# Two weight tiles a visit, in place of one, for the modulation's columns on TensorE

## The chip, the core and the metric

The kernel runs on one core of one Trainium2 chip. The metric is the device time of one execution in microseconds. A core has the engines TensorE (PE; its weight loads are listed apart as PEld), VectorE (DVE), ScalarE (ACT), GpSimd (POOL) and SyncE (SP), which here only issues loads and stores. Each engine works through its own instructions in the order in which they were put down at build time, and semaphores hold an instruction until what it reads is there.

## The reference

A trunk of two layers on 1024 tokens of 1024 channels. Layer 0, in which the change lies, mixes tokens by a Conformer convolution:

```python
c_act = jax.nn.silu(c)
for i in range(DEPTH):
    mod = c_act @ ada_w[i] + ada_b[i]
    sh_m, sc_m, g_m, sh_f, sc_f, g_f = jnp.split(mod, N_ADA, axis=-1)
    h = modulate(rms_norm(x, norm_mix_g[i]), sh_m, sc_m)
    # i = 0: u = a * sigmoid(g) with [a, g] = h @ w1 + b1; causal depthwise
    # convolution of width 31; LayerNorm; silu; @ w2 + b2   (i = 1: pooling)
    x = x + (1.0 + g_m)[:, None, :] * y
    h = modulate(rms_norm(x, norm_ffn_g[i]), sh_f, sc_f)
    x = x + (1.0 + g_f)[:, None, :] * swiglu_ffn(h, ...)
```

`modulate(h, shift, scale)` is h * (1 + scale) + shift. The change is about `c_act @ ada_w[0]` for the last four of the six parts of mod (g_m, sh_f, sc_f, g_f), of 1024 columns each.

## The kernel before, in words

The tokens are worked on in two chunks of 512, A and B. Every large product is made of three products of a high and a low part; a block of 24 products (8 tiles of input channels, 3 products each) makes one output tile of 128 channels by 512 tokens in a PSUM bank. In conv_in, blocks a and g come in turn: a_92 and g_93 (in PE's order by their ids a_715, g_716), then a_127 and g_128 (a_854, g_855), then a_982 with g_983, a_1105 with g_1106, and so on. ScalarE makes t, the sigmoid of a g, DVE multiplies it by a into u, and with that both banks are free again. t_124 is the sigmoid of g_93, t_141 that of g_128. Beside this DVE and GpSimd work through the 31 taps of the depthwise convolution on u: DVE adds its taps up in ca, and for GpSimd ScalarE makes the products pr, which GpSimd adds up in pa; in the end DVE adds pa to ca. There are three buffers for pr.

While chunk A is in conv_in, chunk B's norm is made. TensorE sums the squares (var), DVE takes the reciprocal root (var, col), TensorE spreads it over the partitions (rstd), and for each of eight tiles DVE makes t, ScalarE the high part of h and DVE the low part (h<-t,mod,h). Chunk B's first block, a_1232, reads these eight h three products at a time. rstd_1045 (rstd_1073 in the changed kernel) is norm_b's.

A weight tile is loaded by SP into a raw buffer (`load_weight`, L491; three of these), ScalarE writes its high part and its negative (two instructions, the lines CAST and ACTIVATE w<-raw), and GpSimd issues a load that adds the same weights to the negative (L497), which gives the low part. raw_142 and w_143 are such a tile, raw_147 and w_148 the next.

`ada_columns` (L446) makes the columns of mod. For each of the parts j = 2 and 3 (in conv_in of chunk A and B), then 4 and 5 (from about 206 us), it takes eight weight tiles of 512 KB (adaw, by SP, two buffers). The first operand of a product is a column of c_act 32 wide, so four products that use 32 columns of the array each stand side by side; they add into one bank. A tile is four such instructions, recorded as eight, since a float32 product takes two passes. `columns_done` copies the bank, turns it by two small products (adac) and adds the bias.

What is put down when is decided at build time. A `clock` holds an estimated time for each engine. Between blocks of products, and in the middle of some, `pace` asks the tasks for their next step; a task that said a word of the table `LOAD` is asked again once PE's estimate is that much later. PE's instructions stay in the order in which they are put down; those of the others are ordered by a scheduler from priorities and from what they hang on. A tile's step also issues the load that will take its buffer, so the loads on SP's queue move with the steps.

Of the kernel before, what the change touches and what calls it, by code (L numbers as in the profile page):

```python
# [19 lines left out]
KT = D // P  # L20
# [24 lines left out]
ADA_BUFS = 2  # L45
# [6 lines left out]

PE_TAPS = {6: 15, 7: CW}
DIAGS = 8
LOAD = {"load": 4.0, "slow": 6.0, "next": 4.0, "dots": 4.0}

ON_DVE = (1, 4)
AHEAD = 4
# [73 lines left out]
def trunk(ctx, tc, xT, c, vec, ada, adan, w1f, w1, wdg, w2, wgu, wdn, wds, wpl, out):  # L132
    nc = tc.nc
    ctx.enter_context(tc.manual_schedule(engines={mybir.EngineType.PE}))
    clock = {"PE": 0.0, "V": 0.0, "G": 0.0, "S": 0.0}
# [10 lines left out]
    def matmul(out, lhsT, rhs, start, stop, more=False):  # L146
        n = out.shape[-1]
        clock["PE"] += n / 2400 * (1 if rhs.dtype == F32R else 4) + 0.0025
        last_mm[0] = nc.tensor.matmul(out, lhsT, rhs, start=start, stop=stop, skip_group_check=more).ins.name  # L149
# [55 lines left out]
    def nm(s):  # L205
        uid[0] += 1
        return f"{s}_{uid[0]}"
# [48 lines left out]
    class Task:  # L256
# [6 lines left out]
        def step(self, e):  # L263
            if e != "V" or self.done or clock["PE"] < self.until and not forced[0]:
                return False
            try:
# [3 lines left out]
                if said == "wait":  # L270
                    return False
                if said in LOAD:
                    self.until = clock["PE"] + LOAD[said]
                elif said == "root":
# [31 lines left out]
    def bank(name):  # L306
        return ps.tile([P, 512], F32, tag="mm", name=nm(name))
# [15 lines left out]
    def temp(n, name="t", bufs=0):  # L323
        t = tmp.tile([P, TMPW], F32, tag=name if bufs else "t", name=nm(name), bufs=bufs or 4)
        return t[:, :n]
# [46 lines left out]
    ccols = cst.tile([P, KT, 32], F32, name="ccols")  # L372
# [22 lines left out]
    def ada_load(src, queue=sync):  # L395
        w = raws.tile([P, D], F32, tag="ada", name=nm("adaw"), bufs=ADA_BUFS)
        queue.dma_start(w, src)
        return w
# [45 lines left out]
    Q = D // 4  # L444

    def ada_columns(js):  # L446


        todo = [(j, k) for j in js for k in range(KT)]
        src = lambda j, k: adan[k, :, (j - 2) * D : (j - 1) * D]  # L450
        ws = [ada_load(src(*t)) for t in todo[:ADA_BUFS]]
        for i, (j, k) in enumerate(todo):
            yield "load"
            if k == 0:
                acc = bank("ada")
            w = ws.pop(0)
            for g in range(4):
                matmul(acc[32 * g : 32 * g + 32, :Q], ccols[:, k, :], w[:, g * Q : g * Q + Q], start=k == 0, stop=k == KT - 1)
            clock["PE"] -= 1.3
            if i + ADA_BUFS < len(todo):  # L460
                ws.append(ada_load(src(*todo[i + ADA_BUFS])))
            if k == KT - 1 and (j != 3 or not held[0]):
                yield from columns_done(j, acc)
            elif k == KT - 1:
                held_back.append((j, acc))
# [3 lines left out]
    def columns_done(j, acc):  # L469

        rows = temp(Q)
        S_.copy(rows, acc[:, :Q])
        yield "spread"
        cols = bank("adac")
        for h in range(2):
            matmul(cols[:, 4 * h : 4 * h + 4], rows[:, h * P : h * P + P], quarters, start=True, stop=True)
        m = mod[:, j * KT : (j + 1) * KT]
        V_.tensor_tensor(m.rearrange("p (q h) -> p q h", h=2), cols[:, :KT].rearrange("p (h q) -> p q h", h=2),
                         V("ada_b", j * KT, KT).rearrange("p (q h) -> p q h", h=2), op=ADD)
        ada_gains(0, j, 0, KT, G_)  # L480
        ada_done.add((0, j))
# [1213 lines left out]
    for k in range(KT):  # L1695
# [4 lines left out]
        if k > 1:  # L1700
            acc = squares[0]
# [11 lines left out]
    def ada_pair(k):  # L1713
        w = wts.tile([P, 2, D], F32, tag="w", name=nm("adaw"))
        load_next(w, ada_m[0, k][:, 0:2, :])
        return w

    w = ada_pair(0)
# [7 lines left out]
    for k in range(KT + 1):  # L1726
        if k < KT:
            if k:
                w = ada_pair(k)
# [3 lines left out]
                dots = [V_.last.ins]  # L1733
# [8 lines left out]
        if k < KT:  # L1742
# [7 lines left out]
            t = temp(A.n) if k else first_t  # L1750
# [48 lines left out]
    def ada_first(take):  # L1799
        T["ada", 0] = Task(ada_columns((2, 3)), False, 0)  # L1800
        T["ada", 0].free = True
# [27 lines left out]
    def ada_second(take):  # L1829
        T["ada_f"] = Task(ada_columns((4, 5)), False, 0)  # L1830
        T["ada_f"].free = True
# [214 lines left out]
```

## Time and profile before

| what | value |
| --- | --- |
| time, median of 3 runs | 1695.77 us (1695.59 to 1695.8) |
| the profiled execution, its own time | 1696.16 us |
| its span | 1694.4 us |
| mean granted TensorE clock | 0.998 |
| TensorE busy | 1665.3 us (98%) |
| columns' weight tiles used | from 71.6 to 323.4 us |

The span is from the first to the last instruction of the profiled execution; 1.8 us lie around it. A row of a timeline has the start, the length to the last end, the engine, line and operation, what is written and read, how many instructions in a row it stands for, and in brackets the idle time before it with what ended it. TensorE's instructions overlap, so the end of a row lies after the start of the next.

### The profile page before, as it was taken

What the parts mean: (1) busy time and instruction counts of PE and PEld (TensorE: products, weight loads), DVE (VectorE), ACT (ScalarE), POOL (GpSimd) and SP (SyncE); (2) the same over time, 40 slices, a digit from 0 to 9 for tenths busy, and PEclk for the clock granted to TensorE, in tenths of its full rate; (3) what the DMA queues carried; (4) which work ended last, traced back from release to release, by engine and by line L of the source; (5) the groups of instructions that cost most, each with busy time, mean ns of one, the idle gap of its engine ahead of it and who ended that gap; (6) DMA issues with size and microseconds to landing.
All of it is one profiled execution on the core that took longest, in us unless ns stands there. A gap on an engine that the chain in (4) does not pass through costs nothing.

```text
span 1694.4 us, 21271 instructions
## 1 busy us (share of the span) xinstructions
PE 1665.3 (98%) x7586; PEld 1356.4 (80%) x7586; DVE 1319.9 (78%) x1872; ACT 799.4 (47%) x1085; POOL 486.3 (29%) x566
## 2 busy tenths in 40 slices
PE   7999999999999999999999999999999999999997
PEld 5777777778887888888888888888888888888886
DVE  8889899899758887887665797848777677668657
ACT  3669686866546332333213336646422222234454
POOL 3587767796001111212110222100111111000013
PEclk9999999999999999999999999999999999999999
DMA  8858987828675788886878846877677776586564
GB/s 302 288 172 230 228 237 199 223 79 238 216 240 152 256 261 298 281 259 212 339 267 281 256 149 202 240 245 212 176 233 230 212 222 193 200 273 204 193 166 122
DMA packets 115820, 380.70 MB, mean 225 GB/s; under 512 B 12225, under 2 KB 14401, under 8 KB 115714
## 3 DMA queue, kind: packets, MB, share of 16 engines
q1 hardware_dynamic: 77888, 247.46, 41.3%
q0 software_dynamic: 36736, 130.83, 31.6%
q8 instruction: 60, 0.98, 0.2%
q10 hardware_dynamic: 1090, 1.05, 0.2%
q14 instruction: 46, 0.38, 0.1%
HBM read 311.92 MB, written 63.18 MB: 221 GB/s over the span
## 4 chain that ended last, share of the span: by engine, by line
PE 88%; DVE 5%; DMA 2%; ACT 2%; issue 2%; POOL 1%; DVEq 0%; SPq 0%; ACTq 0%; POOLq 0%
PE a L149 24%; PE dn L149 23%; PE e L149 13%; PE p L149 12%; PE y L149 6%; PE g L149 3%; PE first L149 3%; PE tap L149 2%; POOL pa L126 1%; PE ada L149 1%; DMA adaw<-in_adan_dram 1%; DVE t L126 1%; DVE x L126 1%; PE var L149 1%; DVE ca L126 0%
## 5 line engine op out<-in xcount | busy, mean ns | idle before, releaser
L126 ACT CAST w<-raw 128x1024 fp32r<-128x1024 f32 (+1 forms) x249 | 258.5, 1041 | 332.6 <-PE dn L149 98.6
L149 PE MATMUL dn<-g,w 128*128 128x512 f32 x1152 | 265.4, 391 | 2.3 <-DVE g L126 1.0
L149 PEld LDWEIGHTS dn<-g,w 128*128 128x128 f32 x1152 | 215.4, 188 | 48.7 <-DVE x L126 1.7
L126 DVE TENSOR_TENSOR w<-raw,w 128x1024 fp32r<-128x1024 f32 (+1 forms) x177 | 217.9, 1234 | 41.3 <-ACT w L126 40.8
L149 PE MATMUL a<-n,w 128*128 128x512 f32 x1056 | 247.7, 390 | 1.1 <-DVE n L126 0.7
L149 PE MATMUL p<-h,w 128*128 128x512 f32 x1056 | 244.2, 391 | 0.8 <-DVE h L126 0.6
L126 POOL TENSOR_TENSOR pa<-pa,pr 128x512 f32<-128x512 f32 x160 | 228.2, 1510 | 23.9 <-ACT pr L126 17.8
L149 PEld LDWEIGHTS a<-n,w 128*128 128x128 f32 x1056 | 197.9, 188 | 44.1 <-DVE n L126 2.2
L149 PEld LDWEIGHTS p<-h,w 128*128 128x128 f32 x1056 | 197.4, 188 | 43.7 <-DVE h L126 1.5
L149 PE MATMUL dn<-hi,w 128*128 128x512 f32 (+1 forms) x600 | 173.6, 373 | 0.4 <-DVE w L126 0.4
L126 DVE SCALAR_TENSOR_TENSOR ca<-u,vecs,ca 128x512 f32<-128x512 f32 x245 | 169.9, 748 | 0.5
L126 DVE SCALAR_TENSOR_TENSOR x<-dn,gains,x 128x512 f32<-128x512 f32 (+1 forms) x144 | 100.9, 732 | 35.9 <-PE dn L149 35.9
L149 PEld LDWEIGHTS dn<-hi,w 128*128 128x128 f32 x600 | 109.7, 188 | 20.4 <-DVE w L126 0.9
L149 PE MATMUL a<-t,w 128*128 128x512 f32 x528 | 123.6, 390 | 0.8 <-DVE w L126 0.8
L149 PE MATMUL e<-b,w 128*128 128x512 f32 x528 | 123.4, 389 | 0.6 <-DVE r L126 0.6
L149 PE MATMUL e<-t,w 128*128 128x512 f32 x528 | 123.2, 389 | 0.0
L126 ACT ACTIVATE pr<-u,vecs 128x512 f32<-128x512 f32 x160 | 108.3, 716 | 25.2 <-POOL pa L126 17.6
L1117 POOL DMA_DIRECT2D raw<-in_wgu_dram x41 | 36.3, 884 | 283.9 <-DVE k L126 100.7
L149 PEld LDWEIGHTS a<-t,w 128*128 128x128 f32 x528 | 99.1, 188 | 21.7 <-DVE w L126 1.2
L149 PEld LDWEIGHTS e<-b,w 128*128 128x128 f32 x528 | 99.1, 188 | 21.5 <-DVE r L126 1.1
L149 PEld LDWEIGHTS e<-t,w 128*128 128x128 f32 x528 | 99.2, 188 | 20.5
L149 PE MATMUL dn<-lo,w 128*128 128x512 f32 (+1 forms) x300 | 111.7, 372 | 0.0
(183 smaller groups left out, 2375.2 us busy)
## 6 DMA issues: line engine op xcount, KB each, us to landing
raw<-in_wgu_dram SPq DMA_DIRECT2D x132, 512.0 KB, 4.9
adaw<-in_ada_dram POOLq DMA_DIRECT2D x48, 512.0 KB, 7.4
raw<-in_wdn_dram SPq DMA_DIRECT2D x44, 512.0 KB, 7.9
raw<-in_wgu_dram POOLq DMA_DIRECT2D x41, 512.0 KB, 7.1
raw<-in_w_dram SPq DMA_DIRECT2D x36, 512.0 KB, 6.1
gd<-g POOLq DMA_DIRECT2D x36, 512.0 KB, 7.8
g<-gd SPq DMA_DIRECT2D x36, 512.0 KB, 5.8
kinds<-k POOLq DMA_DIRECT2D x33, 512.0 KB, 7.2
```

The source lines that it names most:

```text
L126: self.last = self.order(getattr(self.eng, name)(out, *args, **kw))
L149: last_mm[0] = nc.tensor.matmul(out, lhsT, rhs, start=start, stop=stop, skip_group_check=more).ins.name
L1117: d = order(nc.gpsimd.dma_start(w[i], wgu[l, fp, src], accum_op=ADD))
```

## The change

A step now takes two tiles, and the next is due 11.0 after it by PE's estimate (the first is due after 4.0, as before). The two loads that follow are issued after both tiles' products. The number of instructions stays: one tap of the convolution goes from DVE to GpSimd, and one subtraction (us) from GpSimd to DVE.

```diff
-LOAD = {"load": 4.0, "slow": 6.0, "next": 4.0, "dots": 4.0}
+LOAD = {"load": 4.0, "both": 11.0, "slow": 6.0, "next": 4.0, "dots": 4.0}
...
-        for i, (j, k) in enumerate(todo):
-            yield "load"
-            if k == 0:
+        for i in range(0, len(todo), ADA_BUFS):
+            yield "both" if i else "load"
+            these = todo[i : i + ADA_BUFS]
+            if these[0][1] == 0:
                 acc = bank("ada")
-            w = ws.pop(0)
-            for g in range(4):
-                matmul(acc[32 * g : 32 * g + 32, :Q], ccols[:, k, :], w[:, g * Q : g * Q + Q], start=k == 0, stop=k == KT - 1)
-            clock["PE"] -= 1.3
-            if i + ADA_BUFS < len(todo):
-                ws.append(ada_load(src(*todo[i + ADA_BUFS])))
+            for (j, k), w in zip(these, ws):
+                for g in range(4):
+                    matmul(acc[32 * g : 32 * g + 32, :Q], ccols[:, k, :], w[:, g * Q : g * Q + Q], start=k == 0, stop=k == KT - 1)
+                clock["PE"] -= 1.3
+            ws = [ada_load(src(*t)) for t in todo[i + ADA_BUFS : i + 2 * ADA_BUFS]]
```

SP's queue, from the third column tile in conv_in on (adaw are the columns' tiles, raw the convolution's weights). Before:

```order
L167 DMA adaw_100_759<-in_adan_dram 128x1024
L491 DMA raw_142_974<-in_w1_dram 128x1024
L491 DMA raw_147_984<-in_w1_dram 128x1024
L167 DMA adaw_121_831<-in_adan_dram 128x1024
L491 DMA raw_211_1433<-in_w1_dram 128x1024
L167 DMA adaw_131_893<-in_adan_dram 128x1024
```

And now:

```order
L167 DMA adaw_100_763<-in_adan_dram 128x1024
L167 DMA adaw_101_765<-in_adan_dram 128x1024
L491 DMA raw_142_974<-in_w1_dram 128x1024
L491 DMA raw_147_984<-in_w1_dram 128x1024
L491 DMA raw_211_1428<-in_w1_dram 128x1024
L491 DMA raw_213_1434<-in_w1_dram 128x1024
```

The fourth column tile went from behind raw_147 to ahead of raw_142; the next one went behind raw_211 and one more.

PE, the second half of the third pair in conv_in of chunk A. Before:

```order
L149 MATMUL g_983<-h_327,w_849 128x512 x3
L149 MATMUL rstd_1045<-ident,col_951 128x128 x4
L149 MATMUL g_983<-h_328,w_849 128x512 x3
L149 MATMUL g_983<-h_329,w_849 128x512 x3
L149 MATMUL g_983<-h_330,w_849 128x512 x3
L149 MATMUL g_983<-h_331,w_849 128x512 x3
L149 MATMUL ada_754<-adaw_944,ccols 32x256 x4
L149 MATMUL a_1105<-h_324,w_858 128x512 x3
```

And now:

```order
L149 MATMUL g_983<-h_330,w_849 128x512 x3
L149 MATMUL g_983<-h_331,w_849 128x512 x3
L149 MATMUL ada_754<-adaw_919,ccols 32x256 x4
L149 MATMUL ada_754<-adaw_921,ccols 32x256 x4
L149 MATMUL rstd_1073<-ident,col_951 128x128 x4
L149 MATMUL a_1101<-h_324,w_858 128x512 x3
```

rstd went from the middle of g_983 to behind it and behind two column tiles.

DVE, the beginning of norm_b (x is the chunk's input, col the last of the reciprocal root, pa_89 GpSimd's sum of taps). Before:

```order
L126 SCALAR_TENSOR_TENSOR col_138_951<-var_137_946,col_138_951 128x4
L126 SCALAR_TENSOR_TENSOR t_153_1050<-x_5_83,gains_263,rstd_152_1045 128x512
L126 SCALAR_TENSOR_TENSOR t_155_1057<-x_5_83,gains_263,rstd_152_1045 128x512
L126 SCALAR_TENSOR_TENSOR t_157_1064<-x_6_84,gains_263,rstd_152_1045 128x512
L126 SCALAR_TENSOR_TENSOR h_108_793<-t_153_1050,mod_262,h_108_793 128x512
```

And now:

```order
L126 SCALAR_TENSOR_TENSOR col_138_951<-var_137_946,col_138_951 128x4
L126 TENSOR_TENSOR ca_118_798<-pa_89_708,ca_118_798 128x512
L126 SCALAR_TENSOR_TENSOR t_156_1078<-x_5_83,gains_263,rstd_155_1073 128x512
L126 SCALAR_TENSOR_TENSOR t_158_1085<-x_5_83,gains_263,rstd_155_1073 128x512
L126 SCALAR_TENSOR_TENSOR u_75_664<-u_75_664,vecs_78,ca_118_798 128x512
L126 SCALAR_TENSOR_TENSOR t_160_1092<-x_6_84,gains_263,rstd_155_1073 128x512
L126 SCALAR_TENSOR_TENSOR h_110_790<-t_156_1078,mod_262,h_110_790 128x512
```

The addition of GpSimd's sum pa_89 went ahead of the first t; before it stood behind the sixth h (h_113). From the first t to the last h there are now 27 instructions on DVE (t_156 to h_117), 25 before (t_153 to h_115).

Elsewhere: in GpSimd's order the last addition into pa_89 is now the twelfth behind w_143's load, before the tenth, with w_148's load among them both times. In ScalarE's order two products pr stood between w_143's two instructions and t_124 before, and three stand there now. In PE's order the two tiles of each of the sixteen steps stand next to each other. From about 345 us on the orders of all engines are the same.

## Prediction

> **What bounds the kernel now.** The page was read first, then TensorE's waits, then the timelines of the stretch in which most of the changed steps stand.
>
> ```profile
> span 1694.4 us, 21271 instructions
> PE 1665.3 (98%) x7586; PEld 1356.4 (80%) x7586; DVE 1319.9 (78%) x1872; ACT 799.4 (47%) x1085; POOL 486.3 (29%) x566
> PE 88%; DVE 5%; DMA 2%; ACT 2%; issue 2%; POOL 1%; DVEq 0%; SPq 0%; ACTq 0%; POOLq 0%
> ```
>
> TensorE is busy for 98% of the span and holds 88% of the chain that ended last. A microsecond taken from its order is a microsecond of the span, unless another engine is then late. So two things are read: what a visit of the columns costs TensorE, and who is nearly late. The list of waits from 60 to 340 us, where all 32 tiles are used (engine, tile, releaser: us in total, times, longest):
>
> ```profile
> PEld ada L149 <- issue: 11.0, 31, 0.4
> PE p L149 <- DVE h L126: 0.6, 2, 0.3
> PE y L149 <- DVE v L126: 0.5, 1, 0.5
> PE ada L149 <- DMA adaw<-in_adan_dram: 1.0, 1, 1.0
> ```
>
> One visit waits for data (1.0 us). The other 31 show only a short hole with no cause, ahead of their weight loads. TensorE's timeline, chunk A's third and fourth conv_in pairs:
>
> ```profile
> 91.38 0.64 PE L149 MATMUL ada<-adaw,ccols 128*32 128x256 f32 x8 [1.02 <-DMA adaw<-in_adan_dram]
> 91.95 1.05 PE L149 MATMUL var<-ones,acc 128*128 128x1 f32 x8
> 92.86 5.69 PE L149 MATMUL a<-h,w 128*128 128x512 f32 x24
> 98.48 0.64 PE L149 MATMUL ada<-adaw,ccols 128*32 128x256 f32 x8
> 99.05 3.02 PE L149 MATMUL g<-h,w 128*128 128x512 f32 x12
> 101.91 1.05 PE L149 MATMUL rstd<-ident,col 128*128 128x128 f32 x8
> 102.72 3.00 PE L149 MATMUL g<-h,w 128*128 128x512 f32 x12
> 105.65 0.64 PE L149 MATMUL ada<-adaw,ccols 128*32 128x256 f32 x8
> 106.22 5.74 PE L149 MATMUL a<-h,w 128*128 128x512 f32 x24
> 111.89 0.64 PE L149 MATMUL ada<-adaw,ccols 128*32 128x256 f32 x8
> ...
> 118.13 0.64 PE L149 MATMUL ada<-adaw,ccols 128*32 128x256 f32 x8
> 118.70 5.74 PE L149 MATMUL a<-h,w 128*128 128x512 f32 x24
> ```
>
> Visits are 6.24 us apart (105.65 to 111.89, and on to 118.13) with 24 products between. 24 products at a steady 0.228 us (in the row at 106.22, 5.74 less the last one's 0.5 of tail, over 23) are 5.47, so a visit costs 0.77 us: 0.57 from its start to the next product, 0.2 in slower products at its edges. The last row begins a_1232, chunk B's first block, which reads norm_b's h. DVE makes these:
>
> ```profile
> 88.81 0.75 DVE L126 SCALAR_TENSOR_TENSOR u<-a,vecs,t 128x512 f32<-128x512 f32 x1 [1.25 <-ACT t L126]
> 103.07 2.06 DVE L126 SCALAR_TENSOR_TENSOR t<-x,gains,rstd 128x512 f32<-128x512 f32 x3 [2.71 <-PE rstd L149]
> 109.80 1.57 DVE L126 SCALAR_TENSOR_TENSOR h<-t,mod,h 128x512 fp32r<-128x512 f32 x1
> 112.11 0.74 DVE L126 SCALAR_TENSOR_TENSOR h<-t,mod,h 128x512 fp32r<-128x512 f32 x1
> 121.62 1.56 DVE L126 SCALAR_TENSOR_TENSOR h<-t,mod,h 128x512 fp32r<-128x512 f32 x1
> ```
>
> The last h is done at 123.18. Its products are the block's last three, from 118.70 + 21 x 0.23 = 123.6. So before, this chain has 0.4 us to spare: TensorE and DVE are level there.
>
> **The change part by part.**
>
> *A visit for two tiles.* Sixteen visits go. The second tile still costs its eight products (two passes of four side by side). The passes' pitch is not in a row; the row gives 0.64 us from the first start to the last end with a product's 0.39 of length in it, so some 0.25 us between the passes, and two more passes cost about 0.44 to 0.5. A pair then costs some 1.21 against 1.54: 0.33 us gained. The bounds are 0 (the second tile costs as much as a visit) and 0.55 (its passes overlap as four side by side do). I take 0.33, since the edges are what the pair has once. Sixteen pairs: 5.3 us, and the wait of 1.02 goes because its load is issued a visit earlier: at most 6.3, or 1689.9 us.
>
> *Two loads in place of one on SP's queue.* The queue moves 512 KB tiles, and is slow here:
>
> ```profile
> 72.27 0.33 SPq L167 DMA_DIRECT2D adaw<-in_adan_dram  x1
> 72.87 3.27 SPq L491 DMA_DIRECT2D raw<-in_w_dram  x2
> 78.51 0.33 SPq L167 DMA_DIRECT2D adaw<-in_adan_dram  x1
> 78.51 12.82 DMA adaw<-in_adan_dram
> DMA to landing us min/median/max: 12.0/12.0/12.0
> DMA to landing us min/median/max: 12.8/12.8/12.8
> ```
>
> The last two rows are the landings of raw_142 (issued 72.87) and raw_147 (75.81): at 84.9 and 88.6; the tile issued at 78.51 lands at 91.33. Landings come in the order of issue, 3.7 and 2.7 us apart. In the new order both columns' tiles stand ahead of raw_142 (the rows of SP's order), so adaw_101 takes its place and raw_142 lands in raw_147's, at 88.6, 3.7 us later. Bounds: 0, if landings did not follow the order of issue, and 6.5 (two places). I take 3.7.
>
> *Who waits for raw_142.* ScalarE, which works in order:
>
> ```profile
> 84.97 1.05 ACT L126 CAST w<-raw 128x1024 fp32r<-128x1024 f32 x1 [1.72 <-DMA raw<-in_w_dram]
> 85.92 1.06 ACT L126 ACTIVATE w<-raw 128x1024 fp32r<-128x1024 f32 x1
> 86.88 1.32 ACT L126 ACTIVATE pr<-u,vecs 128x512 f32<-128x512 f32 x2
> 88.11 0.67 ACT L126 ACTIVATE t<-g,vecs 128x512 f32<-128x512 f32 x1
> ```
>
> It already waited 1.72 us for this tile. Behind it stand the products pr that GpSimd adds up, and t_124, the sigmoid that frees a bank for a_982 and that DVE's u awaits (1.25 us, above). New: casts from 88.7 to 90.6 (two take 1.91), then three pr in place of two (0.62 each, 1.85), t_124 done at 93.1. Without this TensorE would reach a_982 at 92.86 - 1.02 - 2 x 0.33 = 91.2; it starts at 93.1. The gain so far is spent, with 0.2 over.
>
> *rstd_1045 behind g_983 and a pair.* In PE's new order it comes after all of g_983, not half. a_982 takes 5.6, g_983 5.6, the pair 1.21: rstd at 105.5 (before 101.91), done 0.9 later. Without the late raw_142 it would be 103.6.
>
> *DVE's norm_b behind the sum pa_89.* The new DVE order puts ca_118<-pa_89 ahead of the first t of norm_b; before it stood after the sixth h. GpSimd adds:
>
> ```profile
> 87.33 0.87 POOL L497 DMA_DIRECT2D w<-in_w_dram  x1 [2.02 <-ACT w L126]
> 87.94 5.28 POOL L126 TENSOR_TENSOR pa<-pa,pr 128x512 f32<-128x512 f32 x4
> 92.90 1.16 POOL L497 DMA_DIRECT2D w<-in_w_dram  x1
> 93.51 10.98 POOL L126 TENSOR_TENSOR pa<-pa,pr 128x512 f32<-128x512 f32 x8
> ```
>
> Ten additions stand between w_143's accumulating load (87.33) and the end of the last into pa_89, done at about 101.8 (93.51 + 6 x 1.37). The load waits for ScalarE's cast, 3.7 us later now, and by GpSimd's new order twelve additions follow it: 90.6 + 0.6 + 12 x 1.37 + 0.6 = 108.2. DVE's add to 108.9; t_156 starts there, later than rstd allows (106.4), and 5.8 us later than before (103.07).
>
> *The chain to the last h.* Before, 25 DVE instructions from 103.07 to 123.18: 20.1 us. New, 27 by DVE's order, from t_156 to h_117 (the subtraction us_184 and taps of the convolution come in, others go): 20.1 + 2 x 0.72 = 21.5, so 130.4. Bounds: the eight h take 0.74 or some 1.57 (rows at 112.11 and 109.80), as GpSimd works beside them, so 17 to 24.5 us: 126 to 133.4. TensorE comes to those products at 105.5 + 0.8 + 2 x 5.6 + 1.2 + 4.9 = 123.6. It waits 6.8 us (2.4 to 9.8), and is that much later than before from there.
>
> *The other pairs.* Four in chunk B's conv_in: -1.3. Of four around the layernorm of chunk A, three keep 0.33 (-1.0) and one falls in a wait of y for DVE. Of the last four, most goes into p's waits for h (0.6 above): -0.2. Together -2.5. The orders of all engines are the same from about 345 us on, so nothing follows there.
>
> Sum: +6.8 - 2.5 = +4.3. The profiled execution took 1696.16 us (span 1694.4 and 1.8 around it), 0.39 over the median of the runs shown. 1695.77 + 4.3 = **1700.1 us**.
>
> **A rule against the change.** This trace shows TensorE slow after waits, at its start:
>
> ```profile
> 11.60 1.87 PE L149 MATMUL var<-ones,acc 128*128 128x1 f32 x8 [4.79 <-DVE acc L126]
> 15.52 2.05 PE L149 MATMUL rstd<-ident,col 128*128 128x128 f32 x8 [2.05 <-DVE col L126]
> ```
>
> The same eight products take 1.05 us at 91.95 and 101.91. If a wait of 6.8 us at a_1232 did the same, and the block of 24 after it ran at half pace, up to 5.5 us would be added: 1705.6. The wait comes in pieces, as each h is made, so I give it little. [...]
>
> **The rivals.**
>
> *Landings are not pushed back (no late raw_142).* rstd is at 103.6, and the twelve additions end at 104.5, so t_156 starts at 105.2; 21.5 us more: 126.7. TensorE comes at 121.7 and waits 5.0; 126.7 against 123.6 is +3.1, and the other pairs give 2.5 back: +0.6, 1696.4 us, no change. For it: the loads of three queues share the engines, and the place of one tile need not cost a full slot. Against it: the three landings above, in order of issue.
>
> *Faster.* The place is a_1232 again. With raw_142 on time and none of the eight h stretched by GpSimd (17 us), the last h is done at 122.2, and TensorE, there at 121.7, waits 0.5. The wait of 1.02 and the first four pairs then give 1.9 there, the others 2.5: -4.4, 1691.4 us. It decides at about 19 us for the 27 instructions: above that too little is left. For it: the short h at 112.11. Against it: the two long ones, and GpSimd adding without a pause around them.
>
> *The change does nothing.* Excluded: in PE's order all sixteen pairs stand together, with no product between.
>
> **How the numbers follow.** The late chain through raw_142: 0.55, at 1697.5 to 1703, mostly beyond +0.2%. Landings not pushed back: 0.27, 1694 to 1698. Faster: 0.13, 1690 to 1693. The clock on top: 0.05. A measurement tells 0.2% from no change, 3.4 us: below 1692.4 is faster, above 1699.2 slower. Of the first case 0.06 falls within. So faster 0.12, same 0.34, slower 0.54. The range runs from the edge of the faster case, 1692.5, to the long h, 1703.5. The slower case's own range is 1697.5 to 1703.5.
>
> **What would show it.** Right: one visit per two tiles with pairs at about 1.2 us; ACT's wait for raw near 3.7 us longer at 88.6; DVE's first t of norm_b near 109; a_1232 waiting for DVE h, some 7 us in all. Wrong: the cast at 85 still; t at 105; TensorE without holes from 118 to 131; or a pair that costs 1.5.

## The result, and the profile after

The changed kernel takes 1707.41 us (median of six runs, 1706.09 to 1709.03) beside 1696.07 us for the kernel before (six runs on the same chip, 1695.59 to 1697.41). The medians are 11.3 us apart; the ratio is 1.0062, with a 95% interval of 1.0051 to 1.0073. The sign was as forecast, the size was not: 1700.1 us were forecast, and 1703.5 as the upper end. The profiled execution took 1707.64 us.

The head of the page of the changed kernel:

```profile
span 1705.8 us, 21272 instructions
PE 1669.2 (98%) x7586; PEld 1365.4 (80%) x7586; DVE 1316.1 (77%) x1872; ACT 800.2 (47%) x1086; POOL 491.3 (29%) x566
PE 83%; DVE 7%; DMA 2%; ACT 2%; issue 2%; POOL 0%; DVEq 0%; ACTq 0%; POOLq 0%
```

TensorE executes as many instructions as before and is busy 3.9 us longer; the other 7.5 us of the longer span are waits. On the chain that ended last its share went from 88% to 83%, and DVE's from 5% to 7%. The list of TensorE's waits from 60 to 440 us says where (engine, tile, line and releaser; us in total, times, longest):

```profile
PE p L149 <- ACT t L126: 3.2, 1, 3.2
PE a L149 <- DVE h L126: 3.2, 2, 2.0
PE a L149 <- ACT t L126: 2.3, 1, 2.3
PE y L149 <- POOL v L126: 0.8, 1, 0.8
```

The waits of a are in the stretch that the prediction worked through. The one of p, at 335 us, is in none of its steps. TensorE's timeline shows the stretch, with the rows that answer to those of before:

```profile
94.44 8.61 PE L149 MATMUL a<-h,w 128*128 128x512 f32 x24 [2.33 <-ACT t L126]
...
108.43 1.07 PE L149 MATMUL ada<-adaw,ccols 128*32 128x256 f32 x16
109.43 1.16 PE L149 MATMUL rstd<-ident,col 128*128 128x128 f32 x8
110.34 5.74 PE L149 MATMUL a<-h,w 128*128 128x512 f32 x24
115.92 5.60 PE L149 MATMUL g<-h,w 128*128 128x512 f32 x24
121.45 1.07 PE L149 MATMUL ada<-adaw,ccols 128*32 128x256 f32 x16
122.45 4.88 PE L149 MATMUL a<-h,w 128*128 128x512 f32 x19
129.33 0.97 PE L149 MATMUL a<-h,w 128*128 128x512 f32 x3 [2.01 <-DVE h L126]
131.44 1.22 PE L149 MATMUL a<-h,w 128*128 128x512 f32 x2 [1.14 <-DVE h L126]
132.46 0.85 PE L149 MATMUL adac<-quarters,t 128*128 128x4 f32 x4
133.17 8.07 PE L149 MATMUL g<-h,w 128*128 128x512 f32 x24
```

A pair is one row of 16 now. From 110.34 to 122.45 there are two blocks and a pair, 12.11 us, where before the same 48 products and two visits took 12.48: 0.37 gained per pair. Two blocks of 24 take much longer than the usual 5.6 to 5.7: a_982 with 8.61 and g_1233 with 8.07, each right behind a wait. TensorE's busy time by stretch tells why (columns: window, its length, busy time with the instructions, granted clock, DMA share, GB/s):

```profile
92.00:104.00 12.00, 9.66 (x30) 0.72 0.96 268
104.00:128.00 24.00, 23.32 (x127) 1.00 0.26 92
128.00:134.00 6.00, 3.52 (x11) 0.78 0.00 0
134.00:142.00 8.00, 8.00 (x28) 0.74 0.57 131
```

In the kernel before the granted clock is 1.00 in each of these stretches. Here it falls at both waits, to 0.50 from 94.40 to 98.00 us and from 133.00 to 137.00; a block that such a fall slows is said to run at half pace below. The other engines, first ScalarE and then DVE:

```profile
89.97 1.05 ACT L126 CAST w<-raw 128x1024 fp32r<-128x1024 f32 x1 [5.50 <-DMA raw<-in_w_dram]
...
93.72 0.67 ACT L126 ACTIVATE t<-g,vecs 128x512 f32<-128x512 f32 x1
```

```profile
109.37 0.69 DVE L126 TENSOR_TENSOR ca<-pa,ca 128x512 f32<-128x512 f32 x1 [3.86 <-POOL pa L126]
110.62 1.41 DVE L126 SCALAR_TENSOR_TENSOR t<-x,gains,rstd 128x512 f32<-128x512 f32 x2 [0.56 <-PE rstd L149]
```

raw_142 is cast at 89.97 (84.97 before), the sigmoid t_124 that frees a_982's bank is done at 94.39, and DVE starts norm_b at 110.62, after the sum pa_89. This execution entered the stretch 0.83 us later than the one of before: its first block of conv_in starts at 66.87 where before it did at 66.04. The same kernel profiled again (after_again, below) starts it at 65.96, so that this is a difference between executions. The end of a_1232 is marked by the small products adac right behind it. In the kernel before they start at 124.28:

```profile
124.28 0.50 PE L149 MATMUL adac<-quarters,t 128*128 128x4 f32 x4
```

Now they start at 132.46, which is 8.18 us later, or 7.35 without the late start.

### The profile page after: what moved, and what is told of

Same layout as the page of the kernel before. It is cut to its first block, busy times and chain, and to the rows that moved or that the text cites. A ratio compares the mean times of both kernels' runs of the same rounds, so it can differ in the third digit from the quotient of the medians.

```text
span 1705.8 us, 21272 instructions
## 1 busy us (share of the span) xinstructions
PE 1669.2 (98%) x7586; PEld 1365.4 (80%) x7586; DVE 1316.1 (77%) x1872; ACT 800.2 (47%) x1086; POOL 491.3 (29%) x566
## 4 chain that ended last, share of the span: by engine, by line
PE 83%; DVE 7%; DMA 2%; ACT 2%; issue 2%; POOL 0%; DVEq 0%; ACTq 0%; POOLq 0%
PE dn L149 23%; PE a L149 23%; PE e L149 13%; PE p L149 12%; PE y L149 6%; PE g L149 2%; PE tap L149 2%; DVE ca L126 2%; DMA raw<-in_w_dram 1%; PE ada L149 1%; DVE w L126 1%; DMA adaw<-in_ada_dram 1%; DVE t L126 1%; DVE x L126 1%; DVE u L126 1%
```

## The experiments

The theory was the prediction's: the second load ahead of raw_142 makes it late, and the lateness goes through GpSimd's sum and DVE's norm_b to a_1232. To it came what the trace added: the half pace behind the waits, and the wait at 335 us. Rivals were that the pairs cost by themselves, wherever they stand, and that the half pace adds nothing to a path that DVE sets. The differences below are between medians of runs on one chip; behind each stands the 95% interval of the ratio.

**The first call alone, and the second alone.** Pairs for parts 2 and 3, single tiles for 4 and 5, and the other way round:

```diff
+        size = {2: 2, 4: 1}[js[0]]        # first_only; {2: 1, 4: 2} in second_only
...
+            yield "load" if i == 0 or size == 1 else "both"
+            these = todo[i : i + size]
```

> Two tiles a visit in conv_in (parts 2 and 3) only; parts 4 and 5 one tile a visit as before. Theory (raw_142 lands late in conv_in of chunk A, and TensorE pays for that there with waits and slow products): nearly all of the loss stands here, +9 us against before, about 1705. Rival (each pair costs, wherever it stands): half of the loss, +5.5 us, about 1701.5.

> Two tiles a visit from 206 us on (parts 4 and 5) only; conv_in as before. Theory: +1 to +2 us (a wait of some 3 us for t<-p, and one at y, against eight pairs of 0.35 us and shorter waits for h), 1697 to 1698. Rival (each pair costs): +5.5 us, about 1701.5.

The first call alone: 1705.55 us beside 1696.14, +9.4 us (1.0035 to 1.0065). The second alone: 1697.75, +1.6 us (0.9998 to 1.0017). Together they make 11.0 of the 11.3 us. The intervals are some 5 and 3 us wide, and within them the change falls apart into the two with nothing left over. The forecast for these parts was +5.5 (+6.8 at a_1232, -1.3 for the pairs behind it) and -1.2: it is 3.9 short in the first and 2.8 in the second.

TensorE's timeline of second_only, at p in the first feed-forward:

```profile
326.32 8.48 PE L149 MATMUL p<-h,w 128*128 128x512 f32 x36 [3.20 <-ACT t L126]
```

At the fifth block of p TensorE was 3.6 us ahead of the kernel before (320.24 and 323.88); a wait of 3.20 ahead of the sixth takes nearly all of that back. What the sixth block waits for follows from the PSUM banks, which are given out anew as they come free. ScalarE, in the kernel before and then in the changed one:

```profile
325.33 0.35 ACT L126 COPY t<-ada 128x256 f32<-128x256 f32 x1
```

```profile
336.08 1.28 ACT L126 ACT_TABLE_LOAD   x1
337.37 0.60 ACT L126 ACTIVATE t<-p 128x512 f32<-128x512 f32 x1
```

In the program before, the sixth block has the bank of the last part's columns, which ScalarE's copy leaves at 325.68; TensorE comes to it at 326.74. Now the last pair of tiles is used only at 346.41 and that copy comes later still. In the changed program and in second_only the sixth block has the bank of the first p, which ScalarE's t<-p frees: TensorE goes on at 338.02, when this t is done. Ahead of t stand products for the convolution, two casts and a table load. The wait is there in second_only as in the changed kernel (3.21), and not in first_only.

**One load too many, nothing else.** The kernel before, with one more copy of 512 KB on SP's queue between adaw_100 and raw_142, to a tile that nothing reads:

```diff
+                if j == 2 and k == 0:
+                    d = sync.dma_start(dram.tile([P, D], F32, name="unread"), src(2, 0))
...
```

> The kernel before, one tile a visit, with one thing added: a copy of 512 KB from memory to memory on SP's queue between adaw_100 and raw_142, which nothing reads. All else keeps its order. Theory: raw_142 lands about 3.7 us later, ScalarE's cast, t_124 and DVE's u with it; rstd_1045, in the middle of g_983, then waits 2 to 3 us for DVE's col, and TensorE may run at half pace behind it: +3 to +6 us, though no pair is there. Rival (the loads are hidden, the pairs and the order of the visits cost): within 0.5 us of before.

It took 1699.47 us, +3.3 (1.0010 to 1.0029). ScalarE:

```profile
88.40 1.05 ACT L126 CAST w<-raw 128x1024 fp32r<-128x1024 f32 x1 [5.24 <-DMA raw<-in_w_dram]
```

One place in the queue is 3.4 us for raw_142 (84.97 before), near the 3.7 that the landings gave. No pair is in this kernel, and it is slower all the same. How it is slower differs in part from the expectation: the column tile behind raw_147 comes later too, and TensorE waits for it.

```profile
92.27 0.64 PE L149 MATMUL ada<-adaw,ccols 128*32 128x256 f32 x8 [2.02 <-DMA adaw<-in_adan_dram]
...
93.75 7.29 PE L149 MATMUL a<-h,w 128*128 128x512 f32 x24
```

This block, too, takes 7.29 in place of 5.7 behind a wait of 2.02 (granted clock 0.55 from 94.40 to 98.00 us). The 1.0 us of longer wait and the 1.6 us of half pace make up the 2.5 us by which TensorE is late at the end of a_1232 (126.77 in place of 124.28); it does not wait for norm_b there. So the late raw_142 is shown here, but the loss takes another way than in the changed kernel.

**The pairs, with raw_142 in its old place.** As first_only, but a step's second load is issued by a step of its own later:

```diff
+            for n, t in enumerate(todo[i + ADA_BUFS - size : i + ADA_BUFS]):
+                if n:
+                    yield "late"          # 5.0, and 6.0 to the next pair
+                ws.append(ada_load(src(*t)))
```

> Two tiles a visit in conv_in as in first_only, with rstd behind the pair and pa_89's addition ahead of the first t as there, but the second of the two loads is issued later, so that SP's queue has raw_142 in its old place (its name is raw_141 here). Theory: ScalarE's cast comes at 85 again, a_982 does not wait for t_124 and is not slow, the first t of norm_b is at 105 to 106 in place of 110.6; the fourth column tile lands some 2 us after TensorE wants it: 1697 to 1700. Rival (the order of rstd and of pa_89 alone makes the loss): 1704 or more, as first_only.

It took 1699.60 us beside 1696.82, +2.8 (1.0009 to 1.0027), where first_only has +9.4. ScalarE, DVE and TensorE:

```profile
85.35 1.05 ACT L126 CAST w<-raw 128x1024 fp32r<-128x1024 f32 x1 [2.01 <-DMA raw<-in_w_dram]
```

```profile
106.62 1.41 DVE L126 SCALAR_TENSOR_TENSOR t<-x,gains,rstd 128x512 f32<-128x512 f32 x2 [1.09 <-PE rstd L149]
```

```profile
124.39 0.97 PE L149 MATMUL a<-h,w 128*128 128x512 f32 x3 [1.32 <-DVE h L126]
126.08 1.21 PE L149 MATMUL a<-h,w 128*128 128x512 f32 x2 [0.72 <-DVE h L126]
127.09 6.78 PE L149 MATMUL g<-h,w 128*128 128x512 f32 x24
```

The cast is back at 85.35, the wait for t_124 is gone, norm_b starts at 106.62, now held by rstd, and a_1232 waits 2.0 us in all, where first_only has 4.6, and g_1233 starts at 127.09, where first_only has 131.78. The load's place so carries some 6 of the 9.4 us. What is left is a wait of 2.31 us for the fourth column tile, whose load now comes late, rstd after a whole block and a pair, the waits for h, and 1.1 us of slow products in the last row. Two of the tiles are single in this kernel, so it isn't first_only with one load moved and nothing else.

**What the half pace costs.** Products whose results nothing uses fill TensorE's waits: 20 of them with 256 columns ahead of a_982, and 9 and 5 with 512 columns ahead of the last two steps of a_1232.

```diff
+    if (ch.i, p, i, k) == (0, FIRST + 2, 0, 0):              # ahead of a_982
+        for n in range(20):
+            nc.tensor.matmul(st["columns"][:, Q:], wts[i][:, 0, :P], st["h", 0][0][0][:, :Q], ...)
+    if ch.i == 1 and p == KT - 1 - SHARE and i == 0 and k in FILL:    # FILL = {6: 9, 7: 5}
+        for n in range(FILL[k]):
+            nc.tensor.matmul(b[1], wts[i][:, 0, :P], st["h", 1][0][0], ...)
```

In a first attempt with both, the products ahead of a_982 also cleared the columns' sums, so that this run computes other values of the modulation:

> The changed kernel with products that nothing reads, where TensorE waits: 20 of 256 columns ahead of a_982, 9 and 5 of 512 columns ahead of the last two steps of a_1232. If the slow blocks (a_982 in 8.6 us, g_1233 in 8.1) come from TensorE's clock after a wait: both take 5.6 us, and the time falls by 2.5 to 3.5 us against the changed kernel (g_1233's part in full, a_982's mostly hidden since the first t of norm_b waits for pa_89), to 1704. Rival (DVE, GpSimd or loads slow the products): both blocks stay above 8 us and the time does not fall.

It took 1706.95 us, +10.8 (1.0043 to 1.0073): both blocks at the full clock (5.74 and 5.75 us, granted clock 1.00 from 94.40 to 104 and from 133 to 142), and no time gained, where 1704 was expected. Behind the waits of p (3.20 us) and near 562 us (1.99) the clock fell instead, to 0.50 from 334 to 336 us and to a mean of 0.96 from 530 to 570. Then each alone, and both, without the clearing, beside the changed kernel once more:

> The changed kernel once more, to stand beside the three with unread products on the same chip: 1706 to 1708.

> The changed kernel with 20 unread products of 256 columns ahead of a_982 alone. Theory: the clock stays up, a_982 takes 5.6 us in place of 8.6, but the first t of norm_b still waits for pa_89 (about 109), so that a_1232 waits 3 us longer and nearly nothing is left: -0.5 us against the changed kernel. Rival (what TensorE saves stays saved): -3 us.

> The changed kernel with 9 and 5 unread products ahead of the last two steps of a_1232 alone. Theory: g_1233 takes 5.6 us in place of 8.1, and nothing behind it is near late: -2 to -2.5 us. Rival (the slow block has another cause): 0.

> The changed kernel with the unread products at both places. Theory: -2.5 to -3.5 us against the changed kernel, unless another wait behind it drops the clock in its turn, as the wait at p#5 and one near 560 us did in the first run of this kind: then 0 to -2.

| kernel | us, median of 5 | beside before (1696.27) | 95% of the ratio |
| --- | --- | --- | --- |
| after_again | 1707.00 | +10.7 | 1.0049 to 1.0074 |
| fill_a (a_982) | 1707.84 | +11.6 | 1.0052 to 1.0077 |
| fill_b (a_1232) | 1704.11 | +7.8 | 1.0034 to 1.0059 |
| fill_ab | 1707.00 | +10.7 | 1.0053 to 1.0080 |

TensorE's rows, first of after_again, then of fill_b:

```profile
92.93 5.73 PE L149 MATMUL a<-h,w 128*128 128x512 f32 x24 [1.73 <-ACT t L126]
...
131.62 7.75 PE L149 MATMUL g<-h,w 128*128 128x512 f32 x24
```

```profile
93.58 7.26 PE L150 MATMUL a<-h,w 128*128 128x512 f32 x24 [2.46 <-ACT t L127]
...
131.49 5.69 PE L150 MATMUL g<-h,w 128*128 128x512 f32 x24
```

In after_again a_982 goes at the full clock (1.00 from 92 to 100 us; the block takes 5.73, where the changed kernel's first profile has 8.61), and the time is the same; fill_a gains nothing either (raw_142 was late in its profiled execution, with the cast at 90.94). So the half pace at a_982 costs next to nothing: DVE's norm_b, which waits for GpSimd's sum, sets the time there. The one behind a_1232 lies on TensorE's own path: filled, g_1233 takes 5.69 in place of 7.75 (granted clock 1.00 from 128 to 142 us), and the medians differ by 2.9 us (fill_b's five runs reach from 1703.03 to 1704.64, after_again's from 1704.21 to 1708.32). The two profiled executions are 4.0 us apart. Of these 2.3 are there at the first y (245.39 and 247.73), and 1.6 come from a block of y that goes at the full clock in fill_b (5.74 us, 1.00 from 240 to 260) and at half pace in after_again (7.30, a mean of 0.91), so that the fill is not the whole of the difference.

Both fills together gain nothing in the end. When the second layer begins, fill_ab is 3.4 us ahead of after_again (528.46 and 531.82); at the end it is 0.2 us ahead. 1.4 us go at a wait of 2.0 us near 562 us for DVE's w, where fill_b waits 0.6, the rest in pieces at dn near 970 and at 1665 us. Why the wait for w is longer with both fills than with one stays open.

**Two ways to keep the gain.** Pairs only for the last eight tiles of part 3, where nothing is late; and pairs for parts 4 and 5 at a pause of 8.0, so that the columns are done earlier; then both:

```diff
+        for step_size in ((1, 1, 1, 1, 1, 1, 1, 1, 2, 2, 2, 2) if js[0] == 2 else (1, 1, ...)):    # late8
```
```diff
+LOAD = {"load": 4.0, "both": 11, "both4": 8.0, ...}             # s80, pairs in parts 4 and 5 alone
```

> Two tiles a visit only for the last eight tiles of part 3 (four pairs, in conv_in of chunk B, where nothing is late); all other visits as before. If a pair gains what the traces show (0.37 us a pair and nothing lost): -1.3 to -1.5 us against before. Rival (a pair gains nothing by itself): 0.

> Two tiles a visit for parts 4 and 5 only, at a pause of 8.0 in place of 11.0, so that the last visit ends before p#5 takes its bank, and p#5 no longer takes the bank that waits for t<-p. Theory: the wait of 3.2 us at p#5 goes, the eight pairs gain 0.37 us each, and the waits of p for h shrink: 2 to 4 us under before, 1692 to 1694. Rival (the wait at p#5 is not due to the bank): as second_only, 1697.5.

> late8 and s80 together: four pairs in chunk B's conv_in, eight pairs at a pause of 8.0 for parts 4 and 5. Theory: the sum of both, 3.5 to 5.5 us under before, 1690.5 to 1692.5. Rival (a gain in one place is given back later): no better than the better of the two.

late8: 1696.22 us beside 1696.82, -0.6 (0.9989 to 1.0006), not to be told from no change, where 1.3 to 1.5 us of gain were expected. In its trace TensorE is 1.7 us earlier at the small products that turn the columns (180.44, 182.12 before). It entered conv_in 0.16 us earlier, so that its four pairs gain 1.5 us, 0.38 each. The gain of 1.6 us is still there when the second layer begins (519.96 and 521.59), and 0.4 of it at the end: 0.7 us go near 1665 us, where TensorE waits for DVE's w (0.4 us before, 0.8 in late8), the rest in small pieces ahead of it.

s80: 1699.77, +2.9 (1.0010 to 1.0028), where 2 to 4 us of gain were expected. The wait of p is gone, as the account of the banks has it: the sixth block has neither bank there, but one that the small products adac have left. TensorE is 4.4 us ahead of before at the sixth block and 5.0 at dn. It loses that when it comes to dn and to a sum of the next norm, which waits 2.06 us for DVE's acc at 424.12:

```profile
350.84 6.46 PE L149 MATMUL dn<-g,w 128*128 128x512 f32 x27 [1.41 <-DVE t L126]
359.21 0.49 PE L149 MATMUL dn<-g,w 128*128 128x512 f32 x1 [1.91 <-ACT g L126]
360.41 9.90 PE L149 MATMUL dn<-g,w 128*128 128x512 f32 x36 [0.70 <-DVE g L126]
```

dn's operand g comes from ScalarE, behind products for the convolution that wait for GpSimd; that order does not get faster because TensorE is early. Behind both places products are slow besides: the 36 in the last row take 9.90 us, where 36 of dn took 8.32 before, and 15 of dn at 424.65 take 5.60, where 38 took 8.78 at 423.61 before. best: 1698.28, +1.5 (1.0000 to 1.0018), where 3.5 to 5.5 us of gain were expected. No version here is shown to beat the kernel before.

## Why the prediction was right in its first chain and wrong in the size

**What held.** A pair gains 0.37 us (0.33 forecast). raw_142 lands behind two column tiles, and the chain from there to a_1232 is the one of the prediction. after_again enters the stretch at the same time as the kernel before:

| | forecast | after_again | first profile | it, less 0.83 |
| --- | --- | --- | --- | --- |
| cast of raw_142 | 88.7 | 88.46 | 89.97 | 89.14 |
| t_124 done | 93.1 | 92.88 | 94.39 | 93.56 |
| norm_b's first t | 108.9 | 108.44 | 110.62 | 109.79 |
| last h done | 130.4 | 129.84 | 131.39 | 130.56 |
| a_1232's end, later than before | 6.8 | 6.7 | 8.18 | 7.35 |

That single times agree to half a microsecond is in part luck: in the seven kernels with this order of loads the cast comes between 88.46 and 90.94. That the load's place causes most of the lateness is shown by split_first, which is faster with the load put back; before_extra_load shows that one load more makes raw_142 late by 3.4 us. The rival that landings are not pushed back is out with it.

**What failed first: "The wait comes in pieces, as each h is made, so I give it little."** This put the half pace behind a_1232's wait at nothing. The wait does come in pieces (2.01 and 1.14), and the clock falls all the same, at 131.37, for 6.83 us: adac takes 0.85 us in place of 0.50 and g_1233 8.07 where before it took 5.69, 2.7 us in all. With the products that nothing reads in the waits (fill_b) g_1233 takes 5.69 again. The prediction knew the effect, had its bound (up to 5.5 us) and gave it a chance of 0.05. The two rows that it took for products slow after waits, at 11.60 and 15.52, stand ahead of 22.6 us, where in the kernel before the granted clock is first on record and the steady products go from 0.427 to 0.227 us apart for the first time: they show the pace at the start and say nothing of waits in the middle.

**What failed second: "The other pairs … Together -2.5 … nothing follows there."** Of this, the four pairs in chunk B's conv_in do gain (1.5 us in late8's trace). The eight of parts 4 and 5 were put at -1.2; second_only has +1.6 with an interval of -0.3 to +2.9 us that excludes it. Two waits take the gain back in the changed kernel. y waits 0.77, 0.24 and 0.59 us where one of 0.48 was before, and behind them a block goes at half pace (granted clock 0.50 from 257.66 to 261.08 us); the kernel before, then the changed one:

```profile
246.63 0.73 PE L149 MATMUL y<-v,w 128*128 128x512 f32 x2 [0.48 <-DVE v L126]
```

```profile
254.84 0.96 PE L149 MATMUL y<-v,w 128*128 128x512 f32 x3 [0.77 <-POOL v L126]
256.04 0.73 PE L149 MATMUL y<-v,w 128*128 128x512 f32 x2 [0.24 <-DVE v L126]
257.36 7.34 PE L149 MATMUL y<-v,w 128*128 128x512 f32 x24 [0.59 <-DVE u L126]
```

And p waits 3.2 for ScalarE. The orders of all engines are indeed the same from about 345 us on. But which bank a block gets, and so whom it waits for, had changed ahead of that, at a place where the prediction compared orders and did not ask whose bank comes next. The banks are read from the programs, and s80, in which the sixth block of p has another bank, is without the wait.

How much of second_only's +1.6 is which wait stays open. Its profile is of the fastest of its ten executions, 1695.19 us, 1.0 under the median of before: both waits are in it, but the clock stays at 1.00, and it loses nothing on the whole. The other nine took 1697.2 to 1699.9 us, at a mean granted clock of 0.995 to 0.997 in place of its 0.998; that they lost it to half pace would fit this, and no trace shows it.

**The sum, put right** (profiled executions, forecast in brackets): 7.35 at a_1232 (6.8); 2.7 of half pace behind it (0); -2.2 for the seven pairs from there to the first y, 2.8 in the waits of y with their half pace, -3.3 gained from there to p, 3.0 lost at p (-2.5 for these four); 0.8 of late start. That is 11.2 to 11.3, as much as TensorE is late at the sixth block of p (338.02 and 326.74). Behind it the lateness goes to 12.5 us, as the last pair comes there, and back to 11.1 at the second layer, since the kernel before has 1.4 us of waits at dn and the changed one 0.2; the two profiled executions are 11.5 us apart. The range's upper end, 1703.5, held the long h alone, neither the half pace nor a wait in parts 4 and 5.

## What to carry to other kernels

A step that is made larger also moves its loads in one lump: read the queue it shares in order of issue, and price the tile that goes one place back by who waits for it, not by the step's own gain. When a buffer from a rotating pool is held longer, or taken later, the next ones to ask get other buffers: look up for each whose reader frees it, also where the order of instructions is unchanged. And where TensorE is bound and full, waits close together may cost nearly as much again behind them, as those of 2.01 and 1.14 us at a_1232 did with 2.7. A gain on TensorE alone is kept only as far as the next wait for an engine that did not get faster: late8's 1.6 us were down to 0.4 at the end.

## What the runs showed of the hardware that was not expected

The clock behind a wait does not follow from the wait's length. TensorE's block behind a wait of 2.33 us ran at half pace (8.61 us in the changed kernel), behind 2.46 also (7.26 in fill_b, at a mean clock of 0.86 from 92 to 104 us) and behind 2.02 (7.29 in before_extra_load); behind 2.03 (first_only, 5.74), 2.31 (split_first, 5.69) and even 3.20 (second_only, 36 products in 8.48 us) it did not. The same block behind the same wait took 10.04 in after_filled, and in after_again the clock's mean is 0.91 from 326 to 346 us. The three short waits at y, 1.6 us together, brought it on in the changed kernel (7.34 us) and in after_again (7.30); in second_only the same three waits did not (5.74 us at 247.28). Where blocks of 24 were slow behind a wait, they took 6.78 us (g_1233 in split_first) to 8.61 (a_982 in the changed kernel), 1.1 to 2.9 more than the usual 5.7.

A part of this can be read from the trace of the changed kernel. The granted clock is first on record at 25.56 us, where the steady products go from 0.427 to 0.227 us apart. It is 0.50 from 93.82 to 100.65, from 131.37 to 138.20 and from 257.66 to 261.08 us, for 6.83, 6.83 and 3.41 us; each of these six times lies a whole number of 3.413 us behind 25.56 (20 and 22, 31 and 33, 68 and 69 of them). TensorE in two stretches of that length around the wait of 2.33, then in two of first_only around its wait of 2.03 (columns as above):

```profile
90.41:93.82 3.41, 1.70 (x12) 1.00 0.72 258
93.82:97.23 3.41, 2.79 (x7) 0.50 1.01 293
```

```profile
88.59:92.00 3.41, 2.49 (x16) 1.00 0.84 282
92.00:95.42 3.42, 2.31 (x10) 1.00 0.97 296
```

In the changed kernel TensorE stands for 1.7 us of the first stretch, and the clock is down in the next; in first_only it stands for 0.9 and 1.1 us, and the clock stays at 1.00. In the stretches ahead of the other two falls, from 127.96 and from 254.25 us, TensorE stands for 2.4 and 1.4 us. In the one from 336.17, in the wait of p, it stands for 1.9, and the clock is 1.00 in the next. In the kernel before, in stretches of the same length from 22.61 to 1650 us, it stands for at most 1.1 us of a stretch (360.53 to 363.94), and the clock stays at 1.00 throughout. What decides where the clock falls is not shown.
